# Late loads moved to GpSimd's DMA queue, lower weight parts taken off GpSimd, and modulation moved to ScalarE in one transformer layer

## The chip, the cores and the metric

The kernel runs on one core of a Trainium2 chip. The metric is device time in microseconds (us) of one execution. Engines are called as in the profile: PE is TensorE, DVE is VectorE, ACT is ScalarE, POOL is GpSimd, SP is SyncE. Each engine runs its own instructions in order. SP's DMA queue carries almost all loads; POOL and ACT have DMA queues of their own.

## The reference

One layer on x (1 x 512 x 1024) with a conditioning vector c, all in float32:

```python
mod = silu(c) @ w_ada + b_ada
sh_m, sc_m, g_m, sh_f, sc_f, g_f = split(mod, 6)
h = normalize(x) * (1 + sc_m) + sh_m
q, k, v, u, g_sb, g_ssm = split(h @ w_in)
y_sb = stick_breaking_attention(q, k, v) @ w_sb_up
s = gelu(s5(u))
y_ssm = (s * sigmoid(s @ w_glu + b_glu)) @ w_ssm_up
y = (sigmoid(g_sb) * y_sb + sigmoid(g_ssm) * y_ssm) @ w_out
x = layer_norm(ALPHA * x + (1 + g_m) * y, ln1_g, ln1_b)
h = normalize(x) * (1 + sc_f) + sh_f
y = (silu(h @ w_gate) * (h @ w_up)) @ w_ffn_out
out = layer_norm(ALPHA * x + (1 + g_f) * y, ln2_g, ln2_b)
```

Attention has 8 heads of 64, `w_gate` and `w_up` are the two halves of `w_ffn_in` (1024 x 2816 each).

## The kernel before

Every float32 product is made of three fp32r products (`mm3`): high part by high part, high by low, low by high. A tile of weights (128 x 1024, 512 KB) is loaded into one of 8 `raw` buffers; ACT casts the high part (line 178 for `whi`, line 164 for slots), and the lower part, raw minus high, is made in one of three ways (`unit`, `split`): a subtraction on DVE, the same on POOL (both line 159), or, where the engine given is `None`, ACT writes -raw (line 180) and a DMA that POOL issues adds raw to it (line 181). Everything else lives in 53 slots of 128 x 512 (`s`), taken and returned by `get` and `put`. PE's output goes to 8 banks (`b`).

The order of the work on each engine is set by a scheduler that runs a simulated timeline with priorities (`prio`: "first", "ssm", "qkv", "attn", "gates", "feed", "later", "mix", "ffn"). One thing is not free: what goes through `load` (line 146) stays in program order on SP's queue. A load that waits for its destination holds all loads that stand behind it.

The stages, with their place in the trace: the modulated input h and the first products (to about 100 us), the state-space branch with q, k, v (to about 200), attention in 16 half-heads (line 727, to about 320), gelu and the gated unit (`w_glu`, 315 to 337), the up-projections (`w_ssm_up`, `w_sb_up`, to 389), the output projection (`proj`, 389 to 441), the first norm (`ln1_block`, for 4 blocks of 128 rows, 412 to 481), the feed-forward part (from 454), and the last norm (at the end).

The parts that the change touches:

- *Gate tiles.* `gate_tile` makes one of 16 tiles of `h @ w_in` for g_sb and g_ssm; one follows each head half, at low priority, and fills PE while attention waits for DVE and ACT.
- *adaLN pieces.* `later(...)` puts pieces of `mod` that are needed late beside gates 9 to 15, the up-projections and the output projection. The first four go through `ada_gate`: a memset of a slot on POOL, a load of a 1 KB row of `b_ada`, then two 512 KB loads (`ra<-w_ada`) and eight scaled sums on DVE (line 252) onto the slot. Their sum over partitions (`ones`) is made at the start of the projection.
- *Norm weights.* `bcast` loads ln1 and ln2 weights, broadcast to all partitions, 256 KB each.
- *`proj`.* Called for blocks 0, 1 and then 2, 3: loads x (two halves of 256 KB per block), scales one half on POOL (line 921), takes the eight tiles of `w_out` (tiles 0 to 3 are kept in slots for both calls), and multiplies. `ENG` names the engine of each lower part: V is DVE, G is POOL. `FENG` does so for the first four tiles of `w_ffn_in`.
- *`ln1_block`.* Per half h of a block: norm, then `n1`, the normalized x (on ACT for h = 1, on DVE, line 964, for h = 0), a transpose on PE (line 967), modulation (line 972 on DVE, line 974 on ACT, by the table `ME`, entry 2i + h for block i), a cast and a subtraction to the two parts that PE multiplies (`h`).
- *`first_half`.* The first products of the feed-forward part, on the four tiles named by `FENG`.

## Time and profile before

| | |
|---|---|
| median of 3 runs | 823.52 us (823.5 to 823.6) |
| profiled execution | 824.6 us |
| its span | 822.9 us |
| PE, DVE, ACT, POOL busy | 92%, 71%, 53%, 18% of the span |
| granted TensorE clock, mean | 0.968 |

The span runs from the first to the last instruction in the trace; the profiled execution's time has 1.7 us around it. A busy share is an average over all stages. In a timeline, a row is a run of like instructions on one engine, and what stands in brackets is the time that the engine stood idle before it and what released it. A row of a DMA queue (SPq) tells when transfers were issued, not when they landed. The clock is a share of TensorE's upper level: 1.00 is 2.4 GHz, 0.50 is 1.2 GHz.

### The profile page before, as it was taken

To read this page: it belongs to the slowest core of one execution; us is meant where nothing else is said; L and a number is where in the kernel's file an instruction comes from. 1 tells how busy PE (TensorE), PEld (TensorE's weight loads), DVE (VectorE), ACT (ScalarE), POOL (GpSimd) and SP (SyncE) were. 2 spreads that over 40 slices of the span, in tenths; PEclk is the share of its full clock that TensorE was granted. 3 is DMA by queue.
4 is the path that set the end of the run, shared out by engine and by line. 5 is a ranking of instruction groups with operands and counts; after the bars stand their busy time and mean duration, and the time that the engine had idled before them with its cause. 6 is when DMAs were issued, how large, how long until landed. Compare 5 with 4: busy or idle time off the path is not lost.

```text
span 822.9 us, 12321 instructions
## 1 busy us (share of the span) xinstructions
PE 758.1 (92%) x4767; PEld 667.5 (81%) x4767; DVE 586.4 (71%) x975; ACT 438.8 (53%) x715; POOL 148.4 (18%) x161
## 2 busy tenths in 40 slices
PE   4989989999996797999994999999999999999995
PEld 2878879988885676787883989999999999888884
DVE  5798474884658774878799898777787876434267
ACT  4375644678987676761435473534445456532211
POOL 1443244512323221001634000000000000000013
PEclk9999998999997999899998899999999999999998
DMA  9992227964207792925941004414445344440001
GB/s 281 361 242 67 52 64 153 237 137 77 52 10 196 228 232 92 350 70 187 358 120 52 1 19 136 155 53 146 144 143 183 104 139 145 157 148 27 1 26 76
DMA packets 99498, 111.49 MB, mean 135 GB/s; under 512 B 4456, under 2 KB 86384, under 8 KB 99440
## 3 DMA queue, kind: packets, MB, share of 16 engines
q1 hardware_dynamic: 95552, 96.82, 37.1%
q0 software_dynamic: 3744, 13.63, 9.0%
q8 instruction: 37, 0.61, 0.3%
q10 hardware_dynamic: 144, 0.26, 0.1%
q14 instruction: 21, 0.17, 0.1%
HBM read 94.97 MB, written 2.10 MB: 118 GB/s over the span
## 4 chain that ended last, share of the span: by engine, by line
PE 75%; DVE 10%; DMA 6%; issue 3%; ACT 2%; SPq 2%; POOL 1%; POOLq 0%; DVEq 0%; ACTq 0%
PE b L149 74%; DMA ra<-w_ada 3%; SPq L146 2%; DMA s<-w_in 1%; DVE s L252 1%; DVE st L288 1%; DMA raw<-w_glu 1%; DMA wlo<-raw 1%; DVE h L159 1%; DVE s L407 1%; DMA s<-x 0%; DVE s L159 0%; DVE s L972 0%; DVE s L943 0%; DVE s L477 0%
## 5 line engine op out<-in xcount | busy, mean ns | idle before, releaser
L149 PE MATMUL b<-h,whi 128*128 128x256 f32 (+1 forms) x896 | 216.5, 331 | 20.8 <-DVE h L159 9.4
L149 PEld LDWEIGHTS b<-h,whi 128*128 128x128 f32 x896 | 151.5, 191 | 36.5 <-DVE h L159 9.6
L159 DVE TENSOR_TENSOR wlo<-raw,whi 128x1024 fp32r<-128x1024 f32 x103 | 129.6, 1264 | 72.1 <-ACT whi L178 37.1
L149 PE MATMUL b<-s,whi 128*128 128x256 f32 (+1 forms) x800 | 168.5, 308 | 7.6 <-ACT whi L178 6.8
L149 PE MATMUL b<-h,wlo 128*128 128x256 f32 (+1 forms) x448 | 148.2, 331 | 1.4 <-DMA wlo<-raw 1.4
L149 PEld LDWEIGHTS b<-s,whi 128*128 128x128 f32 x800 | 129.7, 190 | 18.0 <-ACT whi L178 6.9
L149 PE MATMUL b<-whi,s 128*128 128x512 f32 (+1 forms) x392 | 122.6, 390 | 0.0
L149 PE MATMUL b<-s,wlo 128*128 128x256 f32 (+1 forms) x400 | 121.5, 306 | 0.0
L159 DVE TENSOR_TENSOR s<-s,s 128x512 fp32r<-128x512 f32 (+4 forms) x112 | 76.4, 689 | 56.4 <-PE b L149 23.0
L178 ACT CAST whi<-raw 128x1024 fp32r<-128x1024 f32 x66 | 69.0, 1048 | 84.7 <-PE b L149 66.5
L1054 ACT CAST whi<-raw 128x1024 fp32r<-128x1024 f32 x70 | 72.7, 1050 | 77.5 <-PE b L149 41.6
L149 PEld LDWEIGHTS b<-h,wlo 128*128 128x128 f32 x448 | 85.8, 192 | 8.9 <-DMA wlo<-raw 1.9
L149 PEld LDWEIGHTS b<-whi,s 128*128 128x128 f32 x392 | 73.2, 188 | 16.6
L149 PE MATMUL b<-s,s 128*128 128x128 f32 (+2 forms) x438 | 81.9, 317 | 2.0 <-POOL s L159 1.4
L164 ACT CAST s<-s 128x512 fp32r<-128x512 f32 (+1 forms) x106 | 57.7, 569 | 41.3 <-DMA s<-w_in 12.1
L149 PEld LDWEIGHTS b<-s,wlo 128*128 128x128 f32 x400 | 75.7, 190 | 3.7
L149 PEld LDWEIGHTS b<-s,s 128*128 128x128 f32 x438 | 68.5, 192 | 11.2 <-POOL s L159 1.6
L149 PE MATMUL b<-wlo,s 128*128 128x512 f32 (+1 forms) x196 | 76.4, 390 | 0.0
L1233 POOL TENSOR_TENSOR s<-s,s 128x512 f32<-128x512 f32 x6 | 8.5, 1430 | 357.1 <-DVE s L1232 357.1
L159 POOL TENSOR_TENSOR s<-s,s 128x512 fp32r<-128x512 f32 (+1 forms) x32 | 40.2, 1264 | 79.0 <-ACT s L164 77.6
L1047 DVE TENSOR_TENSOR raw<-raw,raw 128x1024 f32<-128x1024 f32 x40 | 48.6, 1219 | 4.8 <-DMA raw<-w_ffn_in 4.3
L252 DVE SCALAR_TENSOR_TENSOR s<-ra,ca,s 128x256 f32<-128x256 f32 x88 | 47.2, 557 | 4.0 <-DMA ra<-w_ada 3.2
(246 smaller groups left out, 1096.1 us busy)
## 6 DMA issues: line engine op xcount, KB each, us to landing
raw<-w_ffn_in SPq DMA_DIRECT2D x44, 512.0 KB, 4.5
ra<-w_ada SPq DMA_DIRECT2D x32, 512.0 KB, 7.2
raw<-w_in SPq DMA_DIRECT2D x26, 512.0 KB, 4.7
wlo<-raw POOLq DMA_DIRECT2D x26, 512.0 KB, 5.2
raw<-w_ffn_out SPq DMA_DIRECT2D x22, 512.0 KB, 3.3
wa<-w_ada SPq DMA_DIRECT2D x12, 512.0 KB, 7.6
raw<-w_out SPq DMA_DIRECT2D x12, 512.0 KB, 6.5
s<-x SPq DMA_DIRECT2D x16, 256.0 KB, 3.4
```

The lines of the kernel that those rows point to most:

```text
L146: return tc.keep_in_program_order(nc.sync.dma_start(out=o, in_=i))
L149: return nc.tensor.matmul(o, lhsT, rhs, start=start, stop=stop, skip_group_check=True, **kw)
L159: return eng.tensor_tensor(dst, a, b, ALU.subtract)
L164: acopy(h[:, :n], x[:, :n])
L178: acopy(hi, raw)
L252: stt(dst, r_, ca[:, k:k + 1], init if k == 0 else dst, ALU.mult, ALU.add)
L288: V.bn_stats(st[:, i, :], x)
L407: e.scalar_tensor_tensor(p_, n, -c, p_, ALU.mult, ALU.add)
L1047: tt(r, x, y, ALU.add)
L1054: acopy(hi, x)
L1233: G.tensor_tensor(z[h], z[h], l2b[h], ALU.add)
```

## The change

1. `ENG`: the lower parts of the second call of `proj` go from POOL to DVE. As tiles 0 to 3 stay from the first call, that is three tiles.
2. `FENG` is gone: the first four tiles of `w_ffn_in` get their lower parts as -raw by ACT and an accumulating DMA, which `split` can now do too (`lower`).
3. `ME`: modulation of block 1, half 1 and of block 3, half 1 goes from DVE to ACT.
4. n1 of half 0 goes from DVE to ACT in blocks 1 to 3.
5. `aside`: DMAs on POOL's queue, without program order. The `b_ada` rows of `ada_gate`, the norm weights and the x loads of `proj` go there.
6. In `proj` the x loads stand behind the `w_out` tiles in the program.

```diff
...
 PL = 5
 TAIL = 256
-ENG, FENG = "VGVVVGVGGGGVVGGG", "GGGV"
-XE, BE, ME, HE = "VVVV", "VVVV", "VVAVAAAV", "VVVVVVVV"
+ENG = "VGVVVGVGVVVVVVVV"
+XE, BE, ME, HE = "VVVV", "VVVV", "VVAAAAAA", "VVVVVVVV"
 LAST = 6
 FIRST = 2
 ND = (NF - FIRST) // 2
...
     def load(o, i):
         return tc.keep_in_program_order(nc.sync.dma_start(out=o, in_=i))
+    def aside(o, i):
+        return G.dma_start(out=o, in_=i)
     def mm(o, lhsT, rhs, start, stop, **kw):
         return nc.tensor.matmul(o, lhsT, rhs, start=start, stop=stop, skip_group_check=True, **kw)
...
     def sub(dst, a, b, eng=V):
         return eng.tensor_tensor(dst, a, b, ALU.subtract)
+    def lower(l, x, h, eng):
+        if eng is None:
+            act(l, x, AF.Copy, scale=-1.0)
+            G.dma_start(out=l, in_=x, accum_op=ALU.add)
+        else:
+            sub(l, x, h, eng)
     def split(x, n=512, eng=V, keep=False):
         h, l = get(F32R), get(F32R)
         acopy(h[:, :n], x[:, :n])
-        sub(l[:, :n], x[:, :n], h[:, :n], eng)
+        lower(l[:, :n], x[:, :n], h[:, :n], eng)
         if not keep:
             put(x)
         return h, l
     def unit(view, a, b, eng=V):
         with prio("feed"):
             raw = wp.tile([P, D], F32, tag="raw", name=nm("raw"), bufs=NRAW)
...
             hi = wp.tile([P, D], F32R, tag="whi", name=nm("whi"), bufs=NHI)
             lo = wp.tile([P, D], F32R, tag="wlo", name=nm("wlo"), bufs=NHI)
             acopy(hi, raw)
-            if eng is None:
-                act(lo, raw, AF.Copy, scale=-1.0)
-                G.dma_start(out=lo, in_=raw, accum_op=ALU.add)
-            else:
-                sub(lo, raw, hi, eng)
+            lower(lo, raw, hi, eng)
         return hi.rearrange("p (a b) -> p a b", a=a), lo.rearrange("p (a b) -> p a b", a=a)
     def slot_unit(view, a, b, eng=V):
...
         col = j * D + i * 256
         G.memset(dst, 0.0)
-        load(dst[0:1, :], I["b_ada"][0:1, col:col + 256])
+        aside(dst[0:1, :], I["b_ada"][0:1, col:col + 256])
         ada_acc(dst, w_ada[:, :, col:col + 256], 256, dst)
     def ada_gate_pe(j, i, dst):
...
         g = []
         for i in range(2):
             x_ = get()
-            load(x_, I[name][0:1, i * 512:(i + 1) * 512].partition_broadcast(P))
+            aside(x_, I[name][0:1, i * 512:(i + 1) * 512].partition_broadcast(P))
             g.append(x_)
         return g
...
         pre = exp_table(sig)
         def proj(blocks):
-            for i in blocks:
-                po[i] = [bk.get(), bk.get()]
-                xr[i] = [get(), get()]
-                for h in range(2):
-                    load(xr[i][h], I["x"][i * P:(i + 1) * P, h * 512:(h + 1) * 512])
-                G.tensor_scalar(xr[i][1], xr[i][1], ALPHA, None, ALU.mult)
             for k in range(KC):
                 view, eng = w_o[:, k:k + 1, :], (V, G)[ENG[k + 8 * (blocks[0] // 2)] == "G"]
                 if k >= KEEP:
...
                 elif k not in wo:
                     wo[k] = slot_unit(view, 1, D, eng)
                 later(("out", blocks[0] // 2 * 8 + k))
+            for i in blocks:
+                po[i] = [bk.get(), bk.get()]
+                xr[i] = [get(), get()]
+                for h in range(2):
+                    aside(xr[i][h], I["x"][i * P:(i + 1) * P, h * 512:(h + 1) * 512])
+                G.tensor_scalar(xr[i][1], xr[i][1], ALPHA, None, ALU.mult)
             cut = KC - CUT
             for ks, bs in [([k], blocks) for k in range(cut)] + [(range(cut, KC), [i]) for i in blocks]:
                 for i in bs:
...
             mu, rstd, nmr = norm_stats(z, [pre])
             for h in range(2):
                 n1 = get()
-                if h:
+                if h or i:
                     act(n1, z[h], AF.Identity, bias=nmr, scale=rstd)
                 else:
                     ts(n1, z[h], rstd, nmr, ALU.mult, ALU.add)
...
             for c in (0, FH):
                 view = w_f[:, :, c + P * i:c + P * i + P]
                 if len(first) < 2:
-                    w = unit(view, KC, P, (V, G)[FENG[len(first)] == "G"])
+                    w = unit(view, KC, P, None)
                     w = [[x[:, k, :] for x in w] for k in range(KC)]
                 else:
-                    pair = slot_unit(view, KC, P, (V, G)[FENG[len(first)] == "G"])
+                    pair = slot_unit(view, KC, P, None)
                     wx += pair
                     w = [[x[:, k % 4 * P:k % 4 * P + P] for x in pair[k // 4]] for k in range(KC)]
                 first.append(w)
```

What the scheduler makes of it, at three places. Where a line moved in the file, its number differs by a few.

**SP's queue in the attention.** Rows name destination and source; `raw` are weights of gates, `ra` those of adaLN pieces, `s_425` the slot of the first two pieces. Before:

```order
L146 DMA raw_2572<-w_in 128x8x128
L146 DMA raw_2605<-w_in 128x8x128
L146 DMA s_425_2638<-b_ada 1x256
L146 DMA ra_2641<-w_ada 128x4x256
L146 DMA ra_2647<-w_ada 128x4x256
L146 DMA raw_2744<-w_in 128x8x128
L146 DMA s_425_2638<-b_ada 1x256
L146 DMA ra_2779<-w_ada 128x4x256
L146 DMA ra_2785<-w_ada 128x4x256
L146 DMA raw_2791<-w_in 128x8x128
L146 DMA s_456_2824<-b_ada 1x256
```

Now:

```order
L146 DMA raw_2572<-w_in 128x8x128
L146 DMA raw_2605<-w_in 128x8x128
L146 DMA ra_2641<-w_ada 128x4x256
L146 DMA ra_2647<-w_ada 128x4x256
L146 DMA raw_2744<-w_in 128x8x128
L146 DMA ra_2779<-w_ada 128x4x256
L146 DMA ra_2785<-w_ada 128x4x256
L146 DMA raw_2791<-w_in 128x8x128
L146 DMA ra_2827<-w_ada 128x4x256
```

The four rows from `b_ada` are gone from SP; all else keeps its order, and what stood behind them follows the weights of gate 9 (`raw_2605`) directly.

**PE at the end of the attention.** `whi_3190` and `wlo_3191` are gate 15, `s_514`, `s_515`, `s_517`, `s_518` the two parts of the last attention weights, the products with `ident` transpose the state-space output for gelu. Before:

```order
L149 MATMUL b_72<-h_65,whi_3190 128x512
L149 MATMUL b_72<-h_64,wlo_3191 128x512
L842 MATMUL b_66<-ident,s_163_998 128x128 x4
L842 MATMUL b_67<-ident,s_195_1181 128x128 x4
L842 MATMUL b_68<-ident,s_227_1364 128x128 x4
L842 MATMUL b_69<-ident,s_259_1547 128x128
L149 MATMUL b_70<-s_514_3123,s_469_2863 128x256
L842 MATMUL b_69<-ident,s_259_1547 128x128 x3
L149 MATMUL b_70<-s_515_3124,s_469_2863 128x256
L149 MATMUL b_70<-s_514_3123,s_469_2863 128x256
```

Now, at the same place (`whi_3416` is the first tile of `w_sb_up`):

```order
L849 MATMUL b_67<-ident,s_195_1181 128x128 x4
L849 MATMUL b_68<-ident,s_227_1364 128x128 x4
L153 MATMUL b_70<-s_514_3123,s_469_2863 128x256
L153 MATMUL b_70<-s_515_3124,s_469_2863 128x256
L153 MATMUL b_70<-s_514_3123,s_469_2863 128x256
L153 MATMUL b_70<-s_515_3124,s_469_2863 128x256
L153 MATMUL b_70<-s_517_3129,s_469_2863 128x256
L153 MATMUL b_68<-s_329_2113,whi_3416 128x512
L153 MATMUL b_68<-s_330_2114,whi_3416 128x512
L153 MATMUL b_68<-s_329_2113,wlo_3417 128x512
L153 MATMUL b_68<-s_388_2452,whi_3416 128x512
```

Before, the last products of gate 15 stand right ahead of these transposes. Now that gate is done some 35 rows earlier, among other half-heads, and products of the first up-projection stand between the last ones of attention, ahead of the gated unit.

**POOL and PE in the projection and the first norm.** On POOL before (`wlo` are tiles 5 and 7 of `w_out`, `s_633` and `s_635` are the lower halves of tile 1):

```order
L159 TENSOR_TENSOR s_518_3130<-s_516_3127,s_517_3129 128x384
L921 TENSOR_SCALAR s_621_3750<-s_621_3750 128x512
L921 TENSOR_SCALAR s_623_3755<-s_623_3755 128x512
L159 TENSOR_TENSOR s_635_3788<-raw_3781,s_634_3787 128x512
L159 TENSOR_TENSOR s_633_3784<-raw_3781,s_632_3783 128x512
L159 TENSOR_TENSOR wlo_3820<-raw_3817,whi_3819 128x1024
L159 TENSOR_TENSOR wlo_3832<-raw_3829,whi_3831 128x1024
L921 TENSOR_SCALAR s_659_3950<-s_659_3950 128x512
L921 TENSOR_SCALAR s_661_3955<-s_661_3955 128x512
```

Now:

```order
L150 DMA s_541_3273<-ln_b 128x512
L150 DMA s_654_3825<-x 128x512
L150 DMA s_656_3830<-x 128x512
L150 DMA s_655_3826<-x 128x512
L150 DMA s_670_3973<-x 128x512
L150 DMA s_657_3831<-x 128x512
L150 DMA s_672_3978<-x 128x512
L150 DMA s_671_3974<-x 128x512
L150 DMA s_673_3979<-x 128x512
L163 TENSOR_TENSOR wlo_3810<-raw_3807,whi_3809 128x1024
L935 TENSOR_SCALAR s_655_3826<-s_655_3826 128x512
L163 TENSOR_TENSOR s_629_3774<-raw_3771,s_628_3773 128x512
```

The eight x loads stand on POOL ahead of the first `wlo` and of both halves of tile 1. On PE before, around the transposes of block 0 (`ident`):

```order
L149 MATMUL b_73<-whi_3967,s_601_3635 128x512
L149 MATMUL b_73<-wlo_3968,s_601_3635 128x512
L149 MATMUL b_73<-whi_3967,s_602_3636 128x512
L149 MATMUL b_66<-whi_3967,s_601_3635 128x512
L967 MATMUL b_69<-ident,s_681_4118 128x128 x2
L967 MATMUL b_68<-ident,s_680_4106 128x128 x4
L967 MATMUL b_69<-ident,s_681_4118 128x128 x2
L149 MATMUL b_66<-wlo_3968,s_601_3635 128x512
L149 MATMUL b_66<-whi_3967,s_602_3636 128x512
```

Now, at the end of the projection:

```order
L153 MATMUL b_67<-whi_3969,s_614_3726 128x512
L153 MATMUL b_72<-whi_3969,s_613_3725 128x512
L153 MATMUL b_72<-wlo_3970,s_613_3725 128x512
L153 MATMUL b_72<-whi_3969,s_614_3726 128x512
L974 MATMUL b_68<-ident,s_680_4106 128x128 x4
L974 MATMUL b_69<-ident,s_681_4118 128x128 x4
L974 MATMUL b_68<-ident,s_688_4157 128x128 x4
L974 MATMUL b_69<-ident,s_689_4169 128x128 x4
L153 MATMUL b_73<-h_64,whi_4285 128x256
```

The transposes of block 0, which stood amid the second call's products, follow its last product, with those of block 1, and then the feed-forward part begins.

## Rows read from the trace of the kernel before

**Rows 1.** The page: busy us, share of the span, instructions of each engine
```profile
PE 758.1 (92%) x4767; PEld 667.5 (81%) x4767; DVE 586.4 (71%) x975; ACT 438.8 (53%) x715; POOL 148.4 (18%) x161
```

**Rows 2.** Windows: length; busy of PE, PEld, DVE, ACT, POOL; clock; DMA share; GB/s
```profile
250.00:310.00 60.00, 47.54 (x221) 38.88 (x220) 45.78 (x89) 43.66 (x78) 17.79 (x18) 0.89 0.77 207
260.00:270.00 10.00, 8.42 (x24) 6.49 (x25) 8.17 (x14) 5.71 (x11) 3.96 (x4) 0.60 0.28 53
330.00:340.00 10.00, 9.23 (x29) 7.36 (x30) 8.78 (x13) 7.34 (x9) 0.00 (x0) 0.68 1.10 350
```

**Rows 3.** Timeline of PE: start, length, engine, line, operation, count, [idle before, releaser]
```profile
288.25 0.99 PE L149 MATMUL b<-h,whi 128*128 128x512 f32 x2 [4.74 <-ACT s L706]
...
330.77 0.79 PE L149 MATMUL b<-s,whi 128*128 128x512 f32 x1 [6.78 <-ACT whi L178]
...
388.85 0.39 PE L149 MATMUL b<-s,wlo 128*128 128x512 f32 x1
...
389.08 1.88 PE L149 MATMUL b<-s,ones 128*128 128x512 f32 x4
...
444.38 0.39 PE L149 MATMUL b<-h,whi 128*128 128x256 f32 x1 [3.56 <-ACT h L978]
...
454.32 0.58 PE L149 MATMUL b<-h,whi 128*128 128x256 f32 x1 [9.44 <-DVE h L159]
```

**Rows 4.** Timeline of SP's DMA queue, 170 to 325 us
```profile
170.76 5.33 SPq L146 DMA_DIRECT2D raw<-w_in  x2
...
244.49 0.31 SPq L146 DMA_DIRECT2D s<-b_ada  x1
...
271.38 0.25 SPq L146 DMA_DIRECT2D s<-b_ada  x1
...
322.44 1.30 SPq L146 DMA_DIRECT2D s<-ln_b  x2
...
324.31 0.93 SPq L146 DMA_DIRECT2D raw<-w_glu  x2
```

**Rows 5.** Timeline of POOL, at 244 and at 404 us
```profile
244.15 0.56 POOL L257 MEMSET s<- 128x256 f32 x2 [3.33 <-PE b L149]
...
404.85 2.46 POOL L921 TENSOR_SCALAR s<-s 128x512 f32<-128x512 f32 x1
```

**Rows 6.** Timeline of ACT, 306 to 330 us
```profile
306.13 0.52 ACT L747 ACTIVATE s<-s 128x384 f32<-128x384 f32 x1
...
325.46 2.19 ACT L164 CAST s<-s 128x512 fp32r<-128x512 f32 x4
...
329.68 1.04 ACT L178 CAST whi<-raw 128x1024 fp32r<-128x1024 f32 x1 [1.64 <-DMA raw<-w_glu]
```

**Rows 7.** The line of accumulating DMAs on POOL: ns minimum, median, maximum
```profile
L181 POOL DMA_DIRECT2D wlo<-raw x26: 827/869/1057, 50.9 to 303.6; - x26
```

**Rows 8.** The line of lower parts: ns minimum, median, maximum by engine
```profile
L159 DVE TENSOR_TENSOR wlo<-raw,whi x103: 1203/1224/3422, 330.8 to 780.8; 128x1024 fp32r<-128x1024 f32 x103
...
L159 DVE TENSOR_TENSOR h<-s,h x16: 678/684/2677, 19.0 to 484.4; 128x512 fp32r<-128x512 f32 x16
...
L159 POOL TENSOR_TENSOR wlo<-raw,whi x7: 2388/2791/3382, 398.9 to 438.9; 128x1024 fp32r<-128x1024 f32 x7
...
L159 POOL TENSOR_TENSOR s<-raw,s x4: 1297/1672/1840, 391.3 to 441.3; 128x512 fp32r<-128x512 f32 x4
```

**Rows 9.** Timeline of DVE in the first norm
```profile
421.52 2.27 DVE L293 SCALAR_TENSOR_TENSOR mv<-mv 128x1 f32<-128x1 f32 x1
...
439.17 2.68 DVE L159 TENSOR_TENSOR h<-s,h 128x512 fp32r<-128x512 f32 x1
...
447.56 1.35 DVE L972 TENSOR_SCALAR s<-b,sfx 128x128 f32<-128x128 f32 x4
```

**Rows 10.** The page: DMA issues, count, KB each, median us to landing
```profile
raw<-w_in SPq DMA_DIRECT2D x26, 512.0 KB, 4.7
wlo<-raw POOLq DMA_DIRECT2D x26, 512.0 KB, 5.2
```

## The prediction

> **What bounds the kernel now.** I read the page first: TensorE (PE) is busy 92% of the span [rows 1], so only its gaps, and the stretches at the lower clock beside them, can be won. The windows say where to look: from 250 to 310 us PE is busy 47.5 of 60 [rows 2]. The timeline of PE names the stalls: 4.74 us before 288.25, 6.78 before 330.77, and later 3.56 before 444.38 and 9.44 before 454.32 [rows 3]. Behind that the feed-forward part keeps PE busy almost to the end, and the change touches nothing in it but its first products. So there are two places to win in: the attention with the gated unit behind it (250 to 337), and the first norm (441 to 455).
>
> What releases the first place is read on SP's queue. It issues nothing between 176 and 244.49; then comes a `b_ada` row, and the next pair of these is held until 271.38 [rows 4]. POOL's memset of that row's slot starts at 244.15 after 3.33 us of idle, released by PE [rows 5]: the slot comes free that late. SP keeps program order, so behind one row of 1 KB stand the 512 KB `w_ada` loads and all weights of gates 10 to 15, which are what PE fills the attention's waits with. The same happens behind the `ln_b` rows: the `w_glu` loads are issued at 324.31 [rows 4], and the cast of the weights is released by that transfer at 329.68, while the casts of the unit's other operand begin at 325.46 [rows 6].
>
> **The change part by part.** The profiled execution took 824.6 us, 822.9 of it span; the sum is made against 824.6, and the median of the runs is 1.1 us below it. About 0.2% (1.6 us) is what a measurement of this kernel can tell from no change.
>
> *Loads put aside: attention.* The rows of `b_ada` and of the norms leave SP's queue, so the weights of gates 10 to 15 and the `ra` tiles load as buffers come free, before 244. VectorE (DVE) is busy 45.78 of the 60 us from 250 to 310 [rows 2], so 14.2 is the most that can go, if DVE then runs through; the least is nothing, if it only waits elsewhere. I take 8, a little above the middle: the first adaLN sum still needs its memset, now behind a product that PE ran at about 252, plus two issues on POOL, so it starts near 255. The DVE work between it and the last Exp, some 40 us, then ends near 295 without a wait, and near 302 with part of the waits of now. The last Exp, just before 306.13 [rows 6], so comes 4 to 11 us earlier.
>
> *The gated unit.* From that Exp to the cast at 325.46 ScalarE (ACT) has a chain of 19.3 us that the change leaves alone. What goes is the wait for `w_glu`: 330.77 [rows 3], less 325.46 and 0.6 for the first cast, is 4.7 us. Two things are new on PE. The order puts nine products of the first `w_sb_up` tile into the gap ahead of the unit; one product takes 0.23 (388.85 to 389.08 [rows 3]), so this is 9 x 0.23 = 2.1 us of later work done early. And the gates are used up before the last half-heads, which then wait with nothing between them: I charge 1.3, between 0 and 5, which is one stall like that before 288.25.
> The two together: 8 + 4.7 + 2.1 - 1.3 = 13.5 us. The granted clock was 0.60 from 260 to 270 and 0.68 from 330 to 340 [rows 2], so part of each ran at 1.2 GHz, behind stalls. Where a stall goes its slow stretch should go too, and the unfilled end may bring one back; I leave this at nothing, with 3 us either way.
>
> *The output projection.* PE is busy all through it, from 389.08 to 440.8 (444.38 less its 3.56 [rows 3]), so what leaves SP ahead of `w_out` helps nothing that PE waits for. The `x` loads now stand on POOL, in order, behind the last up-projections (whose slots they take) and ahead of the lower parts that stayed there. The slots come free from about 3 us before the projection. Seven further issues at 0.87 [rows 7] end 3.1 us into it; then a `wlo` of 2.8 [rows 8], a scaling of 2.5 [rows 5] and the lower half of k=1 of 1.7 [rows 8] end at 10.1. PE asks for that half after the sums over `ones` (1.9 [rows 3]) and 33 products of 0.23, at 9.5. That is a stall of 0.6; the longest `wlo` of POOL took 3.4 [rows 8] and there are two more behind it, so I take 1.5, between 0 (plain issues cheaper than the accumulating ones) and 4.5 (each of these operations at its longest, and a transfer waited for). The three `wlo` that go from POOL to DVE, 3 x 1.22 = 3.7 us [rows 8], lie under PE's full stretch and cost nothing; without that cover they would cost the 3.7.
>
> *The first norm.* While POOL computes, DVE's operations are drawn out: 2.27 us for one on 128x1, 2.68 for a subtraction [rows 9] whose median is 0.68 [rows 8]. The first `w_ffn_in` units now get their lower parts from ACT and accumulating transfers, so this goes: 4.1 us for these two. Four modulations of block 1 (1.35 [rows 9]) and one n1 of each later block (0.5) move to ACT, which has room. Against that, the order sets the transposes of blocks 0 and 1 behind the whole projection, where those of block 0 stood in the middle of it. About 18 us of DVE work then lie between PE's last product of the projection and the first of the feed-forward part, where 3.56 and 9.44 of idle stand now [rows 3]. The accumulating transfers (0.87 to issue [rows 7], 5.2 to land [rows 10]) are wanted at about the time that they land. I take 0, between +6 (both excesses, the four modulations and one n1 on the path) and -4 (18 less the 13 of now, and 1 gained).
>
> The last norm's loads cost nothing: they are issued under the feed-forward part, with hundreds of us to spare. The sum is 13.5 - 1.5 + 0 = 12.0: from 824.6 it gives 812.6, from the median of 823.5 it gives 811.5, and I say **812**.
>
> What speaks against loads on POOL: 512 KB issued there land after a median of 5.2 us, on SP after 4.7 [rows 10], with DVE busy most of that time, so I count 0.5 for each, hidden. The Trainium skill, SBUF — State Buffer, section "SBUF: two separate sides", warns that a transfer issued from GpSimd stands still while VectorE runs an operation that takes both of its ports, since its descriptors can't be written then. By that rule each row would land one or more DVE operations late, and the sum would lose some of the 8; the 26 transfers here don't show it.
>
> **The rivals.**
> *Given back (chance 0.18).* DVE and ACT, not the late weights, set the end of the attention; the gates are only used up sooner, and PE waits in the last half-heads instead. Then 4.7 of `w_glu` come in, less 1.5 in the projection and 1 in the norm: 2 us, 821.5, or 819 to 824 with the bounds. For it: ACT's chain of 19.3 us stays, and DVE is busy three quarters of the stretch. Against: the 14 us that DVE stands idle there. If even the 4.7 fail, it is 823.5.
> The Trainium skill, DMA: Bandwidth & Descriptors, section "Issuing engines are not separate DMA queues", says that starting transfers from several engines saves only the time to issue them. By that alone this rival holds; rows 4 speak against it, since they show a queue held up by its order and not by its issues.
>
> *Both places (0.10).* The attention gives its 13.5, the norm its 6 and the clock up to 3: 801 to 806.
>
> *Slower (0.14).* POOL's queue becomes the bound. The row of `b_ada` lands late; DVE, in order, stands on its first sum with the attention's subtractions behind it; later the eight `x` issues hold k=1. It decides once a row lands more than 8 us after its memset: then the gain of 8 is gone and the half-heads wait 5, the projection stalls 4.5 and the norm loses 4, against 4.7 won: 823.5 + 8.8 = 832, and half of it is 828.
>
> *The change doesn't do what it says (0.03).* ACT is in order, and casts that the scheduler left behind the attention's own would come as late as now: 823.
>
> **How the numbers follow.** The forecast has 0.55, with a range of its own of 805 to 818: 811.5 with 3 for the clock, 3 to 4 for DVE, and 3 for the projection, not all at one end. The range for 8 in 10 is 803 to 823: the forecast, three quarters of the case given back, and half of the better one. Faster by over 0.2% (below 821.9) is 0.55 + 0.10 + half of the 0.18 = 0.74. Within 0.2% is the rest of that case and the one without effect, 0.12. Slower is 0.14.
>
> **What would show it.** Right: SP issues `w_in` and `ra` loads before 240 us; the last Exp stands near 298; the unit's first product near 317, released by a cast and not by a `w_glu` transfer; the projection starts near 375, with a PE wait of some 2 us in it that POOL releases; the first product of the feed-forward part comes some 65 us after that start, as now. Wrong: PE's idle time between 250 and 331 is as long as now, or has only moved to the last half-heads; the feed-forward part starts over 70 us after the projection; DVE waits for `b_ada` rows.

## The result and the profile after

The changed kernel takes 830.68 us (829.14 to 832.03, four runs) against 823.51 for the kernel before on the same chip: the ratio is 1.008, with a 95% interval of 1.0057 to 1.0102. It is slower by 7 us where the prediction had 812. The profiled execution took 831.28 us with a span of 829.6, so the sum to explain is 829.6 - 822.9 = 6.7 us.

Two landmarks cut the span: the start of the output projection (the first sum over `ones`) and the first product of the feed-forward part that is followed by more than a few others. The timeline of PE after, with its stalls (start, length, engine, line, operation, count, [idle before, releaser]):

```profile
307.51 0.39 PE L153 MATMUL b<-s,s 128*128 128x256 f32 x1 [1.25 <-ACT s L176]
310.12 1.22 PE L153 MATMUL b<-s,s 128*128 128x256 f32 x4 [2.22 <-POOL s L163]
...
317.88 0.38 PE L153 MATMUL b<-s,s 128*128 128x256 f32 x1 [1.59 <-ACT s L176]
320.22 1.12 PE L849 MATMUL b<-ident,s 128*128 128x128 f32 x4 [1.95 <-ACT s L846]
...
385.50 1.88 PE L153 MATMUL b<-s,ones 128*128 128x512 f32 x4
...
454.24 1.97 PE L974 MATMUL b<-ident,s 128*128 128x128 f32 x8 [15.21 <-ACT s L969]
458.93 0.58 PE L153 MATMUL b<-h,whi 128*128 128x256 f32 x1 [2.72 <-ACT h L985]
```

The projection starts at 385.50, where it started at 389.08 [rows 3]: 3.6 us are won up to there. From there to the span's end it is 444.1 us, against 433.8 before: 10.3 are lost. In that, PE now idles 15.21 us before 454.24, on the transposes of block 1, and 2.72 before 458.93, where it idled 3.56 and 9.44 [rows 3]. The first product of the feed-forward part stands 73.4 us behind the projection's start, and stood 65.2.

On SP's queue after, the weights and `ra` tiles do come early, and so does `w_glu` (286.09, where it was 324.31 [rows 4]). The last two rows matter as well: `w_out` is issued from 356.01 on.

```profile
184.25 0.92 SPq L146 DMA_DIRECT2D ra<-w_ada  x2
...
286.09 7.18 SPq L146 DMA_DIRECT2D raw<-w_glu  x2
...
356.01 0.34 SPq L146 DMA_DIRECT2D raw<-w_out  x1
...
361.20 34.72 SPq L146 DMA_DIRECT2D raw<-w_out  x11
```

Before, four x loads stood on SP ahead of `w_out`, and it was issued behind them:

```profile
376.65 4.84 SPq L146 DMA_DIRECT2D s<-x  x4
381.54 0.42 SPq L146 DMA_DIRECT2D raw<-w_out  x1
```

ACT after: the last steps of the attention, and the table load behind them with which gelu begins; then the row where ACT waits for PE.

```profile
305.48 0.53 ACT L754 ACTIVATE s<-s 128x384 f32<-128x384 f32 x1
...
318.24 1.28 ACT L846 ACT_TABLE_LOAD   x1
...
331.20 1.07 ACT L851 COPY s<-b 128x512 f32<-128x512 f32 x1 [4.22 <-PE b L849]
```

The same table load before:

```profile
317.06 1.28 ACT L839 ACT_TABLE_LOAD   x1
```

So gelu begins 1.2 us later than before. The windows after, the first two cut at the landmarks (length; busy of PE, PEld, DVE, ACT, POOL; clock; DMA share; GB/s):

```profile
0.00:385.50 385.50, 352.47 (x2021) 300.24 (x2022) 278.75 (x582) 250.31 (x436) 111.78 (x147) 0.95 0.63 168
385.50:458.93 73.43, 54.57 (x246) 43.86 (x244) 56.82 (x88) 31.24 (x55) 22.56 (x22) 0.86 0.59 162
250.00:318.00 68.00, 59.31 (x277) 49.91 (x276) 54.99 (x99) 46.32 (x85) 18.91 (x23) 0.87 0.63 174
390.00:400.00 10.00, 9.06 (x50) 7.85 (x49) 9.31 (x11) 3.53 (x5) 8.15 (x5) 0.83 0.91 325
```

And before, cut at the landmarks and for the attention's second half:

```profile
0.00:389.08 389.08, 349.70 (x2022) 296.91 (x2023) 274.13 (x577) 247.05 (x430) 108.01 (x136) 0.96 0.60 161
389.08:454.32 65.24, 52.24 (x247) 42.29 (x245) 59.56 (x86) 28.31 (x48) 30.54 (x17) 0.93 0.53 178
250.00:318.00 68.00, 55.54 (x264) 45.81 (x263) 50.78 (x99) 46.91 (x84) 17.88 (x18) 0.90 0.70 187
```

From 250 to 318 PE is busy longer (59.3 us of 68 against 55.5), at a lower clock (0.87 against 0.90). What ends its stalls has changed. Before, the longest ended on an ACT copy (4.74 before 288.25 [rows 3]), and 3.5 us more on a gate's cast or on the transfer of its lower part. Now the gates are spent, and PE waits in the last half-heads for ACT and POOL, which the rows 307.51 to 320.22 above show.

The first two windows tell idle time from slow products. Up to the projection PE is idle 33.0 us, where it was idle 39.4: 6.4 us of idle did go. But about the same number of products keeps it busy 2.8 us longer, at a lower clock, and 3.6 are left. From there to the feed-forward part it is idle 5.9 us longer and busy 2.3 longer, with the clock at 0.86 in place of 0.93. Over the whole span PE is busy 763.9 us, against 758.1 [rows 1], for the same 4767 instructions. So in this execution 5.8 of the 6.7 us are slower products, and 0.9 is idle time. The two trade against each other where PE is not the limit, as the last section shows, so this is no share of causes.

### The profile page after: what moved, and what is told of

It reads as the page before. It is cut to its first block, busy times and chain, and to the rows that moved or that the text cites. A ratio compares the mean times of both kernels' runs of the same rounds, so it can differ in the third digit from the quotient of the medians.

```text
span 829.6 us, 12355 instructions
## 1 busy us (share of the span) xinstructions
PE 763.9 (92%) x4767; PEld 673.1 (81%) x4767; DVE 580.3 (70%) x965; ACT 448.0 (54%) x732; POOL 146.6 (18%) x180
## 4 chain that ended last, share of the span: by engine, by line
PE 78%; DVE 10%; DMA 4%; ACT 3%; issue 2%; SPq 2%; POOL 0%; POOLq 0%; DVEq 0%; ACTq 0%
PE b L153 77%; DVE s L259 2%; SPq L146 2%; DMA s<-w_in 1%; DVE s L163 1%; DMA raw<-w_ffn_in 1%; DVE wlo L163 1%; DMA raw<-w_in 1%; DVE h L163 1%; DVE s L414 1%; DMA wlo<-raw 1%; DMA s<-x 1%; DVE s L481 1%; ACT s L176 0%; DVE st L295 0%
## 5 line engine op out<-in xcount | busy, mean ns | idle before, releaser
L153 PEld LDWEIGHTS b<-h,whi 128*128 128x128 f32 x896 | 151.8, 192 | 19.9 <-ACT h L985 3.8
L163 DVE TENSOR_TENSOR s<-s,s 128x512 fp32r<-128x512 f32 (+4 forms) x112 | 82.1, 740 | 53.0 <-PE b L153 22.9
L153 PE MATMUL b<-s,s 128*128 128x128 f32 (+2 forms) x438 | 86.6, 328 | 7.1 <-ACT s L176 2.8
L153 PEld LDWEIGHTS b<-s,s 128*128 128x128 f32 x438 | 72.1, 200 | 17.1 <-ACT s L176 3.1
L1054 DVE TENSOR_TENSOR raw<-raw,raw 128x1024 f32<-128x1024 f32 x40 | 48.6, 1219 | 10.3 <-DMA raw<-w_ffn_in 10.0
L150 POOL DMA_DIRECT2D s<-ln_g x4 | 2.3, 567 | 278.8 <-DVE s L163 246.3
L259 DVE SCALAR_TENSOR_TENSOR s<-ra,ca,s 128x256 f32<-128x256 f32 x88 | 48.7, 593 | 3.4 <-issue 3.0
```

The source lines that it names most:

```text
L150: return G.dma_start(out=o, in_=i)
L153: return nc.tensor.matmul(o, lhsT, rhs, start=start, stop=stop, skip_group_check=True, **kw)
L163: return eng.tensor_tensor(dst, a, b, ALU.subtract)
L259: stt(dst, r_, ca[:, k:k + 1], init if k == 0 else dst, ALU.mult, ALU.add)
L1054: tt(r, x, y, ALU.add)
```

## Experiments

Theories, as the expectations name them. **A**: the late loads help a little, and the loss in the first norm comes from the x loads (**A1**: from their place, **A2**: from POOL's queue). **B**: the x loads, which stood on SP ahead of `w_out` and waited for slots, held `w_out` back until the up-projections were nearly done (the hold); without it its lower parts stand ahead of the up-projections' last sums on DVE. **C**: the loss comes only when the x loads meet the other parts. **D**: the accumulating transfers make the loss. In what follows, "start" is the projection's start in the profiled execution, "rest" the time from there to the span's end. Each ratio is to the kernel before as it was timed beside the run (medians of 823.7 to 824.3). Starts and rests are of single executions and good to some 4 us, as the last section shows.

| run | what it is | median us | ratio to before (95%) | start | rest |
|---|---|---|---|---|---|
| before | | 823.5 | | 389.1 | 433.8 |
| the change | | 830.7 | 1.008 (1.0057 to 1.0102) | 385.5 | 444.1 |
| e1 | `b_ada` and norm loads only | 821.0 | 0.9965 (0.9947 to 0.9983) | 381.4 | 434.4 |
| e2 | x loads only | 829.2 | 1.0061 (1.0039 to 1.0084) | 389.3 | 439.2 |
| e3 | compute parts only | 822.3 | 0.9979 (0.996 to 0.9998) | 391.2 | 431.9 |
| e4 | all but x | 818.8 | 0.9936 (0.9912 to 0.996) | 383.7 | 435.2 |
| e5 | all, x late on SP | 827.1 | 1.0034 (1.0019 to 1.005) | 385.4 | 442.1 |
| e6 | all, x early on POOL | 829.6 | 1.0064 (1.004 to 1.0088) | 384.1 | 443.9 |
| e7 | all, no accumulating copies in the norm | 831.7 | 1.0088 (1.006 to 1.0116) | 383.5 | 448.2 |
| e8 | e4, transposes for gelu first | 817.6 | 0.992 (0.9896 to 0.9943) | 383.4 | 432.8 |
| e9 | all, first four x on SP | 820.1 | 0.9951 (0.9922 to 0.998) | 388.3 | 434.2 |
| e10 | e6 with the hold | 822.2 | 0.9975 (0.9954 to 0.9995) | 382.4 | 437.4 |
| e11 | all, `w_out` behind the up sums on DVE | 830.5 | 1.0073 (1.0051 to 1.0094) | 383.2 | 445.7 |
| e12 | e9, transposes for gelu first | 816.9 | 0.9915 (0.989 to 0.9941) | 381.7 | 433.6 |
| e13 | e4 with fewer adaLN sums | 812.1 | 0.9853 (0.983 to 0.9877) | 378.7 | 432.1 |
| e14 | before with fewer adaLN sums | 828.3 | 1.004 (1.0016 to 1.0065) | 393.4 | 434.2 |
| e15 | e8, three pieces later | 824.6 | 1.0004 (0.9988 to 1.0021) | 374.1 | 447.4 |

### Which part loses

**e1, the loads alone.**

```diff
-        load(dst[0:1, :], I["b_ada"][0:1, col:col + 256])
+        aside(dst[0:1, :], I["b_ada"][0:1, col:col + 256])
-            load(x_, I[name][0:1, i * 512:(i + 1) * 512].partition_broadcast(P))
+            aside(x_, I[name][0:1, i * 512:(i + 1) * 512].partition_broadcast(P))
```

> The kernel before with only the b_ada rows of the gate pieces and the norms' weights on POOL's queue. Theory A (the late loads do help the attention, but the order puts adaLN sums on DVE and nine products of the first w_sb_up tile ahead of the attention's end, so that only 3 to 4 us are left of the gain; the loss lies in the norm and is not from here): the projection starts near 385.5, the first product of the feed-forward part 65 us after it as before, 819 to 821 us. Rival B (POOL's queue as such is the loss, wherever loads are put on it): 825 or more. Forecast's own view (the loads give 13 us): 811.

821.0 us. Theory A's value; neither the 811 of the forecast nor the loss of rival B as it was put there. The start is 381.4, 7.7 us sooner than before, where theory A had 385.5; the profiled execution was the fastest of ten. PE is busy 6.6 us less up to there (343.1 against 349.7) and idle 1.2 less, so most of it is the clock.

**e2, the x loads alone.** The eight loads go behind the `w_out` tiles, from `load` to `aside`, as in the change's diff.

```diff
-                    load(xr[i][h], I["x"][i * P:(i + 1) * P, h * 512:(h + 1) * 512])
...
+                    aside(xr[i][h], I["x"][i * P:(i + 1) * P, h * 512:(h + 1) * 512])
```

> The kernel before with only the eight x loads of the projection moved behind the w_out tiles and onto POOL's queue. Theory A (the x loads, late on POOL, delay block 0 and with it the scheduler's order of the first norm): 825 to 830, with a longer stretch from the projection's end to the first product of the feed-forward part than the 13.5 us of before. Rival C (the loss comes only when the x loads meet the other parts): 823 to 825. Attention unchanged under both: projection starts at 389.

829.2 us: theory A. The x loads lose 5 us by themselves, all behind the start.

**e3, the compute parts alone.** `ENG`, `FENG`, `ME` and n1 as in the change, all loads as before.

> The kernel before with only the parts that move no plain load: lower parts of the second w_out call on DVE, those of the first four w_ffn_in tiles by ACT and accumulating DMA, more modulation and n1 on ACT. If freeing POOL takes away DVE's drawn-out operations on the path: 817 to 820. Theory A (the accumulating copies stand in ACT's queue on buffers that PE still reads, with the norm's own steps behind them): no gain or a loss, 823 to 828. Attention unchanged: projection starts at 389.

822.3 us, a gain of 0.2% whose interval just leaves out zero. Neither the 817 to 820 of the one view nor a loss.

**e4, all but x.** The change, with the x block of `proj` as it was.

> The whole change with the x loads left on SP ahead of w_out. Theory A (x is what pushes block 0 and 1's transposes behind the projection): projection starts near 385.5, those transposes stand inside it again, 818 to 823. Rival D (the accumulating transfers are the loss in the norm): 828 to 831, as the whole change.

818.8 us, 12 less than the whole change. SP and PE of e4 (x goes out in the hold from 371.38, `w_out` behind it at 376.69; then the projection's start, the transposes of blocks 0 and 1, the first product of the feed-forward part):

```profile
371.38 5.25 SPq L146 DMA_DIRECT2D s<-x  x4
376.69 0.43 SPq L146 DMA_DIRECT2D raw<-w_out  x1
...
383.65 1.88 PE L153 MATMUL b<-s,ones 128*128 128x512 f32 x4
...
429.51 1.03 PE L975 MATMUL b<-ident,s 128*128 128x128 f32 x8
...
434.33 1.04 PE L975 MATMUL b<-ident,s 128*128 128x128 f32 x8
443.25 0.58 PE L153 MATMUL b<-h,whi 128*128 128x256 f32 x1 [7.88 <-ACT h L986]
```

The transposes are back inside the projection, and the waits behind it are 7.88 and, before 448.70, 4.65. The loss is due to x: 12 us here, though only 5 by itself (e2). So theory C is right in part; what adds the other 7 was not taken apart.

**e7, without the accumulating copies.** `unit` and `slot_unit` of the first `w_ffn_in` tiles get POOL and DVE again.

```diff
-                    w = unit(view, KC, P, None)
+                    w = unit(view, KC, P, (V, G)[FENG[len(first)] == "G"])
...
-                    pair = slot_unit(view, KC, P, None)
+                    pair = slot_unit(view, KC, P, (V, G)[FENG[len(first)] == "G"])
```

> The whole change, with the lower parts of the first four w_ffn_in tiles back on POOL (three) and DVE (one). Theory A (the x loads are the loss, the accumulating copies add little): 827 to 832. Rival D (ACT's copy waits for a buffer that PE still reads, with the norm's Ln and Exp behind it: 4.4 and 2.6 us were seen idle there): 822 to 826.

831.7 us. ACT's wait on a buffer that PE still reads was there in the change, but is not what loses; rival D falls.

### What it is about the x loads

**e5, late place, SP's queue**, and **e6, early place, POOL's queue**:

```diff
 e5: x loads behind the w_out tiles
-                    aside(xr[i][h], I["x"][i * P:(i + 1) * P, h * 512:(h + 1) * 512])
+                    load(xr[i][h], I["x"][i * P:(i + 1) * P, h * 512:(h + 1) * 512])
 e6: x loads ahead of the w_out tiles
-                    load(xr[i][h], I["x"][i * P:(i + 1) * P, h * 512:(h + 1) * 512])
+                    aside(xr[i][h], I["x"][i * P:(i + 1) * P, h * 512:(h + 1) * 512])
```

> The whole change, with the x loads behind the w_out tiles in the program but on SP's queue instead of POOL's. Theory A1 (what hurts is the place: the kept w_out tiles take the slots that come free first, x gets those of the last up-projections, and the scheduler sets block 0 and 1's transposes behind the projection): 827 to 832, like the whole change, with the first product of the feed-forward part more than 65 us after the start of the projection. Rival A2 (POOL's queue, in order, with its lower parts behind eight x issues): 818 to 821, like the change without x.

> The whole change, with the x loads on POOL's queue but at their old place ahead of the w_out tiles, so that x has the early slots. Theory A1 (place and slots): 818 to 823. Rival A2 (the queue): 827 to 832.

827.1 and 829.6: both lose, so neither the place alone nor the queue alone is the cause. The queue has a share: late on SP (e5) is 3.6 us faster than late on POOL (the change), and the intervals do not meet. What they share with the change and e2, and not with e4, is that nothing stands ahead of `w_out` on SP, which is issued from 353 to 356 in all of them and from 376.69 in e4. That gave theory B, and the next three.

**e9, only the first four x loads back on SP.**

```diff
+            if blocks[0] == 0:
+                ... x loads by load, ahead of the w_out tiles
...
+            if blocks[0]:
+                ... x loads by aside, behind them
```

> The whole change, but the four x loads of blocks 0 and 1 back on SP ahead of w_out; those of blocks 2 and 3 stay on POOL, behind the tiles. Theory B (the x loads ahead of w_out held w_out back until the up-projections were nearly done; without them w_out comes 20 us earlier and its lower parts stand ahead of the up-projections' last sums on DVE): these four loads are enough, 817 to 821, DVE's last up-projection split within 6 us of the projection's start. If x on POOL hurts through POOL's queue, the other four still do: 823 to 828.

820.1 us: four loads make the difference. DVE's last split of the up-projections is done 6.8 us after the start, near the 6 expected, in a profiled execution that was the slowest of five (824.2).

**e10, the hold without the transfer.** e6, and for each x load a load of a quarter of one row on SP into the same slot.

```diff
+                    load(xr[i][h][0:1, 0:256], I["x"][i * P:i * P + 1, h * 512:h * 512 + 256])
                     aside(xr[i][h], I["x"][i * P:(i + 1) * P, h * 512:(h + 1) * 512])
```

> The whole change with x on POOL in its early slots, and in place of each x load a load of one quarter row (1 KB) on SP into the same slot, ahead of w_out: the hold without the transfer. DVE's order of w_out's lower parts is that of the change without x again. Theory B alone: 818 to 822. If what hurts is that x itself comes late on POOL (behind its issues, with scaling and k=1's lower half behind it): 826 to 830. The order still has the transposes of blocks 0 and 1 behind the projection here, so a time between, near 824, is what both together would give.

822.2 us against the 829.6 of e6, whose program differs by nothing else. SP of e10: the small loads wait for their slots to 370.09, and `w_out` behind them to 374.43.

```profile
370.09 4.29 SPq L146 DMA_DIRECT2D s<-x  x4
374.43 0.36 SPq L146 DMA_DIRECT2D raw<-w_out  x1
```

In e6 `w_out` is issued at 354.57. The last split of the up-projections on DVE, and PE at the start and at the end of the projection:

```profile
389.18 0.68 DVE L163 TENSOR_TENSOR s<-s,s 128x512 fp32r<-128x512 f32 x1
```

```profile
382.36 1.88 PE L153 MATMUL b<-s,ones 128*128 128x512 f32 x4
...
448.03 1.97 PE L976 MATMUL b<-ident,s 128*128 128x128 f32 x8 [14.90 <-ACT s L971]
452.71 0.58 PE L153 MATMUL b<-h,whi 128*128 128x256 f32 x1 [2.72 <-ACT h L987]
```

That split is done 7.5 us after the start, and so it was before:

```profile
395.94 0.68 DVE L159 TENSOR_TENSOR s<-s,s 128x512 fp32r<-128x512 f32 x1
```

In the change it is done at 399.2, 13.7 us after, and 15.4 after in e6; the DVE rows further down show why. The transposes still stand behind the projection here, 14.90 us of idle ahead of them, and the rest is 2.2 us longer than e4's. So the hold is most of the loss, 7.3 of the 10.8 us between e6 and e4. x itself is not late in e6, where the first four loads are issued on POOL from 372 to 381, and that does not save it. What the remaining 3.4 us are is open; the x loads of blocks 2 and 3, which e10 issues only from 396.7, are one candidate.

**e11, the crowding of DVE alone.** The lower parts of `w_out` on DVE are queued behind the last split of the up-projections.

```diff
+        uplast = lows[-1:]
...
+                    with after(uplast):
+                        wo[k] = slot_unit(view, 1, D, eng)
```

> The whole change, with w_out's lower parts on DVE queued behind the last split of the up-projections; x still late on POOL, w_out still loaded early. Theory B in its narrow form (only the crowding of DVE counts): 819 to 823, the last up-projection split within 6 us of the projection's start. If the lower parts then come too late for the first products and PE waits for them, or POOL's late lower half of k=1 is what sets block 0: 825 to 831.

830.5 us: theory B in this narrow form falls. DVE and PE of e11:

```profile
387.50 3.90 DVE L163 TENSOR_TENSOR s<-s,s 128x512 fp32r<-128x512 f32 x2
391.33 1.21 DVE L163 TENSOR_TENSOR wlo<-raw,whi 128x1024 fp32r<-128x1024 f32 x1
392.46 7.17 DVE L163 TENSOR_TENSOR s<-raw,s 128x512 fp32r<-128x512 f32 x5
```

```profile
394.27 2.08 PE L153 MATMUL b<-s,s 128*128 128x512 f32 x4 [3.96 <-DVE s L163]
```

The up-projections' splits are done sooner, but the lower parts come after them, drawn out while POOL computes its own (7.17 us for five that take 0.7 each), and PE waits 3.96 us for them. So what the hold gives is not this one order on DVE. That ACT, DVE and POOL meet `w_out` when the up-projections are nearly through is the reading that is left; no run shows it apart. Why the scheduler sets block 1's transposes where it does was not taken further.

### The attention

**e8, the products of `w_sb_up`.** In e4, the first nine are held behind the last transposes for gelu.

```diff
-                fm_one([x[:, :, m * P:(m + 1) * P] for x in w], attnT, 4, o)
+                with after(trs[-1:] if i == 0 else []):
+                    fm_one([x[:, :, m * P:(m + 1) * P] for x in w], attnT, 4, o)
```

> The change without x, with the first nine products of w_sb_up held behind the last transposes for gelu. If these nine products delay the gated unit (they wait for a bank, and the last transposes stand behind them): 2 to 4 us less than the change without x, 815 to 817. If the unit's operand isn't what ends last there, or the nine products only change places with the same idle: the same, 818 to 820.

817.6 us: 1.3 less than e4, with intervals that overlap. Not settled, though no loss.

**e12.** e9 with the same.

> The first of these with the nine w_sb_up products also held behind the last transposes for gelu. If both hold: 816 to 819, the fastest of all; if the order of those products makes no difference, as the first of these.

816.9 us, the lowest median of a kernel that computes the reference's function: 0.9915 of before (0.989 to 0.9941). Its interval and e8's overlap, so the two cannot be told apart.

**e13 and e14, fewer sums.** They leave out six of the eight scaled sums of each late adaLN piece, in e4 and in the kernel before.

```diff
+            if n == 256 and k % 4:
+                continue
```

> The change without x, leaving out six of the eight scaled sums of each late adaLN piece on DVE (all loads stay). If DVE's sums set the attention's end: the table load for gelu starts at 306 to 311 instead of 319, and the time falls to 806 to 812. If ACT and PE set it: it stays at 316 to 319, 815 to 818 (the sums taken out elsewhere may still give a little).

> The kernel before, leaving out the same sums. If its attention's end is set by the loads held on SP and not by DVE: the table load stays at 315 to 317, 818 to 823. If DVE sets it there too: 306 to 311, 810 to 815; then the late loads were never what the attention waited for, and the forecast's reading of SP's queue was wrong.

Windows and ACT of e13:

```profile
250.00:310.00 60.00, 54.67 (x269) 43.75 (x269) 35.07 (x61) 45.18 (x83) 17.05 (x21) 0.99 0.68 198
```

```profile
315.29 1.28 ACT L849 ACT_TABLE_LOAD   x1
```

DVE is busy 35 us of the 60 instead of 50, and still the table load comes only 4 us sooner than e4's (319.25), between the two expectations. In all seventeen traces it stands between 315.3 and 321.0, and where the late loads still wait on SP (before, e2, e3, e14) it stands between 316.1 and 318.7. So the held loads do not set the attention's end, and DVE's sums are a part of it; what sets the rest is not shown. Of the 6.8 us that e13 gains on e4, 4.9 lie before the start. e14 has less work than the kernel before and is slower by 0.4%: the table load is at 316.07, but the gated unit starts at 335.05 instead of 330.77, behind 7.27 us of idle. The table load is where the first expectation had it, and the time is where neither had it; why the unit waits longer is open.

**e15, three pieces later.** adaLN pieces 4 to 6 move from gates 13 to 15 to the up-projections.

```diff
-LATER = {**{("gate", i): 1 for i in range(9, 16)}, **{("up", i): 1 for i in range(4)}, ("out", 0): 1}
+LATER = {**{("gate", i): 1 for i in range(9, 13)}, **{("up", i): 2 for i in range(4)}}
```

> The change without x, with the products held behind the gelu transposes, and with adaLN pieces 4 to 6 moved from gates 13 to 15 to the up-projections (two per tile there, none in the output projection). If DVE's sums set the attention's end: table load at 310 to 314, the projection starts 3 to 6 us sooner, 811 to 815, unless the sums crowd the up-projections' own work as w_out's lower parts did, then 818 to 825. If they do not: table load unchanged, 818 or more.

824.6 us: the table load moves to 315.42 (319.45 in e8), no further, and the projection pays, as the second branch said (two of its four sums over `ones` wait until 379.60, and PE waits 4.08 later; the start of 374.1 in the table is that of the first two). This is the same as before within the interval.

## Why the prediction was wrong

The forecast was 12.0 us faster and the profiled execution is 6.7 slower. Of the 18.7 us between them, 9.9 lie before the projection's start (13.5 to be won, 3.6 came) and 8.8 behind it (1.5 to be lost, 10.3 came).

**The loads put aside: right about the queue, wrong about what they end.** SP issues `w_in` and `ra` from 184 on, as forecast, and `w_glu` no longer releases anything. But the 8 us taken from DVE's idle time did not come: gelu's table load is at 318.24 and was at 317.06. The step that failed is "the least is nothing, if it only waits elsewhere. I take 8". It read 14.2 us of idle on one engine as time that the stretch could give back, without asking which chain would end last once the gates were there. Taking away three quarters of DVE's adaLN work (e13) moved the table load by only 4 us. The rival "given back" described this, with a chance of 0.18, but for its 4.7 us of `w_glu`, which did not come either. The chain "that the change leaves alone" was misread too. The row at 306.13 [rows 6] is an Exp ahead of the Ln in the last half-head (L747); the last Exp (L767) stands at 316.06. Between them ACT waits 5.2 us for PE and DVE. From that row to the table load it was 10.9 us, and it is 12.8 from 305.48 now.

**The gated unit: up to the projection 3.6 us came in all.** For the unit alone I had 5.5. The unit's first product starts at 331.49, 0.7 us later than before, and not 5 sooner. Up to it PE is idle 6.4 us less, but busy 7.1 longer: 2.1 for nine products more, and 5.0 for slower ones. The fourth transposes stand behind the nine products of `w_sb_up` that I had counted as 2.1 us of gain; ACT waits 4.22 us for them at 331.20. What is won behind it is those nine products, 2.1, and the clock: 0.68 from 330 to 340 before [rows 2], 0.89 now, 2.1 us. 2.1 + 2.1 - 0.7 = 3.5, the 3.6 measured.

**The clock**, of which the prediction said "I leave this at nothing, with 3 us either way", took 2.8 us up to the projection in this execution, inside the 3. Behind the projection's start slower products took 3.0 more, for which the sum had no term. The mean granted clock is 0.953 in it, 0.955 to 0.965 in the other three, and was 0.968 before.

**The output projection: the size right, the reason not.** I took 1.5 lost; from its start to the idle before 454.24 it is 53.5 us, against 51.7: 1.8. Of this, 0.94 is a wait of PE before 398.67 for an adaLN sum on DVE (L259), and the rest is slower products. POOL after:

```profile
383.64 3.70 POOL L150 DMA_DIRECT2D s<-x  x7 [2.96 <-PE b L153]
387.35 2.41 POOL L163 TENSOR_TENSOR wlo<-raw,whi 128x1024 fp32r<-128x1024 f32 x1
391.85 1.70 POOL L935 TENSOR_SCALAR s<-s 128x512 f32<-128x512 f32 x1 [2.09 <-DMA s<-x]
393.53 1.27 POOL L163 TENSOR_TENSOR s<-raw,s 128x512 fp32r<-128x512 f32 x1
...
399.19 1.29 POOL L163 TENSOR_TENSOR s<-raw,s 128x512 fp32r<-128x512 f32 x1
```

Seven x issues took 3.70 us, 0.53 each, not the 0.87 of the accumulating kind that I used. The lower half of k=1 is done at 394.8 and 400.5, 9.3 and 15.0 us after the start, and I had 10.1. PE did not wait for POOL: the order had put the other products first, so that block 0's two halves end 8 us apart (DVE takes them up at 407.41 and 415.42, and before at 412.49 both). As I read it, the lateness so went into the norm and not into a stall; no run shows this apart.

**What I did not price at all: `w_out` coming early.** The sentence that failed is "what leaves SP ahead of `w_out` helps nothing that PE waits for". That is so, but the x loads did something on SP besides: waiting for their slots, they kept `w_out` behind them until 381 us. Now it is issued from 356, and its casts and lower parts meet the up-projections' last steps. DVE after, around the projection's start, while POOL runs the rows above:

```profile
386.98 3.08 DVE L259 SCALAR_TENSOR_TENSOR s<-ra,ca,s 128x256 f32<-128x256 f32 x1
...
395.01 2.86 DVE L163 TENSOR_TENSOR s<-s,s 128x512 fp32r<-128x512 f32 x1
...
398.54 0.68 DVE L163 TENSOR_TENSOR s<-s,s 128x512 fp32r<-128x512 f32 x1
```

A sum of 0.47 us takes 3.08, a split of 0.68 takes 2.86, and the last split ends at 399.2. This is the drawing-out of [rows 9], now among the last steps of the up-projections. e10 shows the worth of the hold: 7 us. It does not show that the drawing-out is the reason, and e11 speaks against DVE's order alone.

**The first norm.** POOL's contention is gone from it as forecast: the subtraction that took 2.68 [rows 9] is now two in 1.24. I took 0 for the stage, with -4 as the worst; 17.9 us of idle replace 13.0, and from the end of the projection (439.03) to 458.93 it is 19.9, against 13.5: 6.4 lost. The 18 us of DVE work were seen and came; what failed is the +6 set against them. In the 15.21 us, ACT's n1 of block 1 waits for statistics that DVE makes at 450.04, behind an addition that waited for a `w_ffn_in` load (e10 has the same):

```profile
448.89 1.23 DVE L1054 TENSOR_TENSOR raw<-raw,raw 128x1024 f32<-128x1024 f32 x1 [1.62 <-DMA raw<-w_ffn_in]
450.04 0.28 DVE L296 BATCH_NORM_AGGREGATE mv<-st 128x2 f32<-128x12 f32 x2
```

My own sign of error, over 70 us from the start of the projection, came true: 73.4. The sum of the parts is -3.6 + 1.8 + 6.4 + 2.1 behind the first product (the lower clock among it) = 6.7.

**The slower rival** had the time (828 to 832) and POOL's queue, but not the mechanism. The memset is at 250.04 and the sum at 252.91, so the first rows were on time. DVE idles 3.00 us before 273.33, five after the second pair's issue, with no releaser named: at most 3 us, under the 8 that it was to decide from.

The rule of the Trainium skill on transfers issued from GpSimd (SBUF — State Buffer, "SBUF: two separate sides") is neither shown nor ruled out here. The `wlo` transfers land after a median of 5.3 us, 5.2 before [rows 10]. The x loads, for which I counted 0.5 us more on POOL, land after 8.3 there, and landed after 3.6 on SP before:

```profile
s<-x POOLq DMA_DIRECT2D x8, 256.0 KB, 8.3
s<-x SPq DMA_DIRECT2D x8, 256.0 KB, 3.6
```

But they now go out among the `w_out` loads (DMA share 0.91 from 390 to 400): late on SP (e5) they take 5.6, and early on POOL (e6) 4.1. No wait of PE or DVE names x or `b_ada`; POOL waits 2.09 us for x before 391.85. By the other rule of the Trainium skill (DMA: Bandwidth & Descriptors, "Issuing engines are not separate DMA queues"), moving a load between queues saves the time to issue it and no more. e10 against e6, 7 us by eight 1 KB loads on SP, shows that the order within a queue is worth more than the issues.

## What to carry to other kernels

Before a load leaves a queue that keeps program order, ask what it holds back: a load that waits for its buffer also times everything behind it, and one freed may send work ahead to engines that are full. Idle time of one engine is the most that a stretch can give, not what it gives: name the chain that ends last once the wait is gone, here the attention's own last half-heads with no gate left to fill them. Where a scheduler orders by a simulated timeline, try the parts of a change apart; here one part lost more than all others won.

## What was not expected of the hardware

The clock differs between executions of the same order. PE's instructions stand in one order in e1 and in the change up to 335 us. The same products of `w_sb_up` follow stalls of the same length (1.24 and 1.22 us); in e1 they are 0.23 us apart and in the change 0.43. PE of e1, and of the change:

```profile
325.37 0.39 PE L153 MATMUL b<-s,wlo 128*128 128x512 f32 x1
325.60 0.64 PE L153 MATMUL b<-s,whi 128*128 128x512 f32 x2
```

```profile
327.12 0.63 PE L153 MATMUL b<-s,wlo 128*128 128x512 f32 x1
327.55 1.05 PE L153 MATMUL b<-s,whi 128*128 128x512 f32 x2
```

The window from 320 to 330 has a granted clock of 0.80 in e1 and 0.50 in the change, that is 1.2 GHz throughout. Up to the unit's first product this makes 3.8 us (327.73 in e1, 331.49 in the change), and e1's ten runs lie between 817.5 and 823.2, with mean clocks from 0.965 to 0.975. Up to there PE is busy 9.0 us longer in the change than in e1 and idle 5.2 less: in the attention, slower products partly fill time in which PE would have waited. So starts and rests of single executions above are good to some 4 us, and the conclusions rest on differences above that, or on the medians.

DVE is drawn out only while POOL computes: in the traces before and after, each DVE operation that takes 60% and 0.3 us more than the median of its group (30 and 34 of them) overlaps a computing instruction of POOL.

A plain transfer issues on POOL in 0.53 us and an accumulating one in 0.87, which no row of before could tell.
